# Gate and up projections of an fp32 decoder layer by Strassen's seven products in place of eight, on one core

## The chip, the cores and the metric

The kernel runs on one core of a Trainium2 chip. The metric is the device time of one execution in microseconds (us). Before the change the median of three runs is 1079.65 us (1079.23 to 1080.08). Engines: PE (TensorE, matmuls and transposes), DVE (VectorE), ACT (ScalarE), POOL (GpSimd), SP (SyncE, which issues the DMAs of the kernel before).

## What is computed

One layer of a decoder on 1024 tokens of width 1024, all in fp32; the channel mixer has 2816 columns.

```python
h = x * (1 + sc1) + sh1
z = h @ w_in + b_in
y = concat([short_conv, pooling, conformer, S5](z)) @ w_o
x = layer_norm(ALPHA * x + (1 + g1) * y, ln1_g, ln1_b)
h = x * (1 + sc2) + sh2
f = (silu(h @ w_gate) * (h @ w_up)) @ w_down
x = layer_norm(ALPHA * x + (1 + g2) * f, ln2_g, ln2_b)
```

The six vectors sc1 to g2 come from a small product with the conditioning vector (`ada`). Layer norms reduce over the 1024 columns of a token.

## The kernel before

**Products.** An fp32 operand is held as two fp32r parts: `split` (L80, L81) makes the high part with an ACT cast and the low part with a DVE subtraction. `passes` (L130 to L132) multiplies two such operands in three matmuls: high by high, high by low, low by high. A matmul is 128 rows by 128 by 512 columns wherever gate, up and down are concerned, and one instruction each.

**Tiles.** The tokens go in two halves of 512 (c = 0, 1). Gate and up have 22 tiles f of 128 columns. `gate_up(c, f, h2)` loads and splits two weight tiles (`gu_pairs`), multiplies both with the modulated input h2 over all 8 row blocks of 128 (`gu_mm`: 2 x 8 x 3 = 48 matmuls into two PSUM banks), and `gu_act` takes silu of one (L593, ACT) times the other (L594, DVE) and splits the result into an act tile that stays in SBUF until the down projection. `down(c)` multiplies 22 act tiles with w_down into eight PSUM banks (528 matmuls).

**Order.** Most of the program is written inside `in_order(ON_PE)`, so PE works in the order of the text; a scheduler sets the order of the other engines by their inputs and priorities. The first half's output projection and norm (`ln1(0, t)`, t = 0 to 3, token tiles of 128) come first. Then gate and up tiles 0 to 10 of the first half (GU_FIRST = 11) run on PE while DVE makes the 31 conformer taps (L408) and other mixers of the second half, T3 = 8 taps per tile. The second half's output projection follows (`out_proj1`, eight PSUM banks, `res1` L529 and L530 reads them), then tiles 11 to 14 of the first half, one ahead of each `ln1(1, t)`, and 15 to 21, then `down(0)`, the 22 tiles of the second half, and `down(1)`.

**ln1.** Statistics on DVE (L476, L479), 1 / deviation by a chain of ten small operations on POOL (`rsqrt`, L376 to L394, and L537), the normalised rows r on ACT (L539), eight transposes on PE (L546) into two PSUM banks, and eight 128-wide ACT operations (L556) that scale and shift them into the next input. For c = 0 the result is split into h2 at once; for c = 1 it goes to DRAM (h2_d) and is loaded and split ahead of the second half's tiles. `keep_x1` scales r (L567, L568) and stores it for `res2`.

**Buffers.** Loads go through four 4 KB-a-partition tiles (tag `raw`); `tmp` has three. Weight pairs (`pr`) rotate through a list; big tiles share space by tag (`ha`, `hb0` to `hb7`, `y0` to `y7`, `m0` to `m5`).

## Time and profile before

| what | value |
|---|---|
| median of 3 runs | 1079.65 us |
| span of the profiled execution | 1076.1 us |
| PE busy | 1040.0 us (97%) |
| DVE busy | 609.1 us (57%) |
| ACT busy | 328.4 us (31%) |
| POOL busy | 142.2 us (13%) |
| DMA issues by POOL | none |

The span is 3.55 us below the median of the runs; the difference lies around the span and is taken to stay. Matmuls overlap, so the time that one costs is read from start to start, not from its own duration. A share of busy time is an average over stages. [...]

### The profile page before, as it was taken

Reading aid. Unit: us, or ns where it says so; the run is one execution under the profiler, and the core shown is the slowest. Engines: PE = TensorE matmul, PEld = TensorE weight load, DVE = VectorE, ACT = ScalarE, POOL = GpSimd, SP = SyncE. Lnnn points to the kernel's source line nnn. Section 1 sums busy time; section 2 is a strip of 40 time slices with the busy share of each in tenths; the row PEclk is TensorE's granted clock in tenths of the full one; section 3 lists DMA queues with packets and bytes.
Section 4 is the critical chain, followed back from the end, with each engine's and each line's share of the span. In section 5 each row is a group of like instructions: output and inputs, shape, how many; then the busy total and the mean of one; then the engine's idle time right before and its main releaser. Section 6 shows DMA issues by size and latency. Waiting matters only on the chain.

```text
span 1076.1 us, 12408 instructions
## 1 busy us (share of the span) xinstructions
PE 1040.0 (97%) x4744; PEld 846.5 (79%) x4744; DVE 609.1 (57%) x921; ACT 328.4 (31%) x462; POOL 142.2 (13%) x447
## 2 busy tenths in 40 slices
PE   8959999999999999999999999999999999999995
PEld 7747777678888888888788888888888888888884
...
DMA packets 53963, 145.23 MB, mean 135 GB/s; under 512 B 9296, under 2 KB 17520, under 8 KB 53904
## 3 DMA queue, kind: packets, MB, share of 16 engines
...
q8 instruction: 37, 0.61, 0.2%
...
## 4 chain that ended last, share of the span: by engine, by line
PE 67%; POOL 9%; DVE 8%; issue 8%; DMA 5%; ACT 2%; SPq 0%; DVEq 0%; POOLq 0%; ACTq 0%
PE mm L131 20%; PE mm L130 19%; PE mm L132 19%; DMA raw<-in_w_ada_dram 2%; POOL s L855 2%; POOL s L862 2%; PE sm L130 2%; PE sm L131 2%; PE sm L132 2%; DMA raw<-in_w_up_dram 2%; DVE raw L168 1%; PE sm L1119 1%; POOL rs_a L376 1%; ACT tmp L556 1%; DVE pr L81 1%
## 5 line engine op out<-in xcount | busy, mean ns | idle before, releaser
L81 DVE TENSOR_TENSOR pr<-raw,pr 128x1024 fp32r<-128x1024 f32 (+1 forms) x161 | 192.1, 1196 | 268.7 <-ACT pr L80 268.3
L130 PE MATMUL mm<-h,pr 128*128 128x512 f32 (+1 forms) x736 | 281.9, 383 | 0.0
L131 PE MATMUL mm<-h,pr 128*128 128x512 f32 (+1 forms) x736 | 280.8, 382 | 0.2 <-DVE h L81 0.2
L132 PE MATMUL mm<-h,pr 128*128 128x512 f32 (+1 forms) x736 | 279.8, 380 | 0.6 <-DVE pr L81 0.5
L80 ACT CAST pr<-raw 128x1024 fp32r<-128x1024 f32 (+1 forms) x161 | 164.9, 1027 | 368.8 <-PE sm L132 130.2
L132 PEld LDWEIGHTS mm<-h,pr 128*128 128x128 f32 x736 | 138.3, 188 | 28.6 <-DVE pr L81 1.5
L130 PEld LDWEIGHTS mm<-h,pr 128*128 128x128 f32 x736 | 138.3, 188 | 27.8 <-issue 0.5
L131 PEld LDWEIGHTS mm<-h,pr 128*128 128x128 f32 x736 | 138.4, 188 | 26.8 <-issue 0.5
L376 POOL TENSOR_SCALAR rs_a<-lmv 128x1 f32<-128x1 f32 x16 | 12.0, 750 | 697.4 <-DVE lmv L479 695.9
L130 PE MATMUL mm<-pr,act 128*128 128x512 f32 x240 | 94.3, 393 | 0.0
L132 PE MATMUL mm<-pr,act 128*128 128x512 f32 x240 | 94.2, 392 | 0.0
L131 PE MATMUL mm<-pr,act 128*128 128x512 f32 x240 | 94.1, 392 | 0.0
L408 DVE SCALAR_TENSOR_TENSOR acc<-up,pack,acc 128x512 f32<-128x512 f32 x120 | 85.0, 747 | 0.0
L594 DVE TENSOR_TENSOR tmp<-tmp,mm 128x512 f32<-128x512 f32 x44 | 30.1, 685 | 71.5 <-PE mm L132 65.1
L168 DVE SCALAR_TENSOR_TENSOR raw<-raw,cond 128x1024 f32<-128x1024 f32 x48 | 58.0, 1222 | 15.8 <-DMA raw<-in_w_ada_dram 15.8
L593 ACT ACTIVATE tmp<-mm 128x512 f32<-128x512 f32 x44 | 26.2, 600 | 118.8 <-PE mm L132 118.8
L131 PE MATMUL mm<-h_a,pr 128*128 128x512 f32 x104 | 42.7, 411 | 13.7 <-DVE h_a L81 13.7
L132 PEld LDWEIGHTS mm<-pr,act 128*128 128x128 f32 x240 | 45.0, 188 | 10.3
L131 PEld LDWEIGHTS mm<-pr,act 128*128 128x128 f32 x240 | 45.1, 188 | 10.3
L130 PEld LDWEIGHTS mm<-pr,act 128*128 128x128 f32 x240 | 45.0, 188 | 10.2
L130 PE MATMUL mm<-h_a,pr 128*128 128x512 f32 x104 | 42.9, 413 | 2.1 <-ACT h_a L80 2.1
L132 PE MATMUL mm<-h_a,pr 128*128 128x512 f32 x104 | 42.1, 405 | 0.0
...
## 6 DMA issues: line engine op xcount, KB each, us to landing
raw<-in_w_ada_dram SPq DMA_DIRECT2D x48, 512.0 KB, 5.0
raw<-in_w_gate_dram SPq DMA_DIRECT2D x44, 512.0 KB, 3.3
raw<-in_w_up_dram SPq DMA_DIRECT2D x44, 512.0 KB, 3.4
raw<-in_w_down_dram SPq DMA_DIRECT2D x44, 512.0 KB, 3.2
raw<-in_w_o_dram SPq DMA_DIRECT2D x16, 512.0 KB, 3.4
raw<-in_w_inB_dram SPq DMA_DIRECT2D x10, 512.0 KB, 3.5
raw<-in_x_dram SPq DMA_DIRECT2D x8, 512.0 KB, 3.2
x_d<-r SPq DMA_DIRECT2D x8, 512.0 KB, 3.5
```

The source lines that it names most:

```text
L80: S.copy(hi, src)
L81: V.tensor_tensor(out=lo, in0=src, in1=hi.bitcast(F32), op=SUB)
L130: PE.matmul(o, wh, xh, start=first, stop=False)
L131: PE.matmul(o, wh, xl, start=False, stop=False)
L132: PE.matmul(o, wl, xh, start=False, stop=last)
L168: V.scalar_tensor_tensor(out=w, in0=w, scalar=1.0, in1=cond, op0=MUL, op1=MUL, accum_out=mod[:, j:j + 1])
L376: G.tensor_scalar(out=a, in0=v, scalar1=EPS, scalar2=None, op0=ADD)
L408: V.scalar_tensor_tensor(out=o, in0=u, scalar=dww[:, i, j:j + 1], in1=o, op0=MUL, op1=ADD)
L593: S.activation(g[:, :CH], z[0], AF.Silu)
L594: V.tensor_tensor(out=g[:, :CH], in0=g[:, :CH], in1=z[1], op=MUL)
L855: i = e.tensor_tensor(out=o, in0=a, in1=b, op=op)
L862: self.eng(o).tensor_scalar(out=o, in0=a, scalar1=s1, scalar2=s2, op0=op0, **kw)
```

## The change

For gate, and likewise for up, let A be the weights of two column tiles (2j, 2j+1) by the two halves of the 1024 rows, and B the two halves of the rows by the two halves of the tokens. Four blocks of output take eight block products; the change takes seven (the Winograd form). A block product for gate and up together is 2 x 4 x 3 = 24 matmuls.

- **On the first half of the tokens:** `c11(j)` takes two of the products, p1 = A11 x B11 and A12 x B21. Their sum is the first half's tile 2j, whose act goes to DRAM (`act_d`). ACT copies p1 out of PSUM between the two products (L616), in the middle of an accumulation, and it is stored (`p1_d`). Tiles 2j + 1 of the first half are not computed here. `c11` runs for j = 0 to 7 ahead of the second half's output projection (GU_FIRST = 8, CF = 6, T3 = 10) and for j = 8 to 10 ahead of `ln1(1, 0)` to `ln1(1, 2)`.
- **When the second half has its norm:** `strassen(j)`, j = 0 to 10, takes the other five products (s1 x t1, s4 x B22, s2 x t2, s3 x t3, A22 x t4; 120 matmuls). `a_ops` loads four weight tiles and makes the sums of weights on DVE (L685) and five split operands; DVE combines p1 and PSUM into the three other blocks (L710 to L730), reading a bank in the middle of its accumulation; acts go to DRAM.
- **Sums of inputs:** `ln1(1, t)` makes the split operands t1 and B22 itself (`tb`), loading B11 from DRAM, and stores t1. `t_ops` loads inputs and t1 back from DRAM and makes t2, t3 and t4 (12 operands, 12 subtractions and 12 splits) behind the first two products of j = 0.
- **Around it:** acts of both halves are loaded from DRAM in the down stage (`down_ops`), the scaling of x1 moves there (`keep_x1`), and x_d, h_d, t_d, p_d and act_d are written by 64 DMAs that POOL issues. SP issues 346 DMAs (317 before). The g, b rows move later, h_b becomes two tiles.

128x512 matmuls: 4144 before, 3880 after. DVE TENSOR_TENSOR operations: 548 and 811. ACT casts: 258 and 318, copies 22 and 48.

```diff
-GU_FIRST = 11
-CF = 8
-T1, T2, T3 = 6, 2, 8
+GU_FIRST = 8
+CF = 6
+T1, T2, T3 = 6, 2, 10
...
     def ln1(c, t, r, h2):
...
         S.activation(r, r, AF.Identity, scale=rs, bias=nb)
+        G.dma_start(x1_d[c * 4 + t], r)
...
-        if c == 1:
-            SP.dma_start(h2_d[:, :, tt].rearrange("k p t -> p k t"), hv)
+        G.dma_start(h2_d[:, :, c * CH + t * P:c * CH + (t + 1) * P].rearrange("k p t -> p k t"), hv)
+        if c == 1:
+            b11 = raw_p.tile([P, 1024], F32, name="raw", tag="raw", bufs=4)
+            bv = b11[:, :CH].rearrange("p (k t) -> p k t", k=4)
+            SP.dma_start(bv, h2_d[:4, :, t * P:(t + 1) * P].rearrange("k p t -> p k t"))
+            V.tensor_tensor(out=bv, in0=hv[:, :4], in1=bv, op=SUB)
+            split(tb[0][:, :4, 0, tt], tb[0][:, :4, 1, tt], bv)
+            split(tb[1][:, :, 0, tt], tb[1][:, :, 1, tt], hv[:, 5:])
+            split(tb[0][:, 4, 0, tt], tb[0][:, 4, 1, tt], hv[:, 4])
+            G.dma_start(t1_d[:, :, tt].rearrange("k p t -> p k t"), bv)
...
+    def product(o, w, m, b, first, last, hs=slice(0, CH)):
+        for k in range(4):
+            ks = slice(512 * m + k * P, 512 * m + (k + 1) * P)
+            xh, xl = B[b][k]
+            passes(o, (w[:, 0, ks], w[:, 1, ks]), (xh[:, hs], xl[:, hs]), first and k == 0, last and k == 3)
+    def c11_mm(w, z, p1, q, lo=0, n=CH):
+        hs = slice(lo, lo + n)
+        for i in range(2):
+            product(z[i][:, hs], w[i], q, ("11", "21")[q], q == 0, q == 1, hs)
+            if q == 0:
+                S.copy(p1[:, i * CH + lo:i * CH + lo + n], z[i][:, hs])
+    def c11_act(j, z, p1):
+        G.dma_start(p1_d[j].rearrange("p a t -> p (a t)"), p1)
+        g = tmp()
+        S.activation(g[:, :CH], z[0], AF.Silu)
+        V.tensor_tensor(out=g[:, :CH], in0=g[:, :CH], in1=z[1], op=MUL)
+        G.dma_start(act_d[2 * j][:, :CH], g[:, :CH])
...
+    def t_ops():
...
+        for k in range(4):
+            a, b = [raw_p.tile([P, 1024], F32, name="raw", tag="raw", bufs=4) for _ in range(2)]
+            SP.dma_start(a[:, :CH], t1_d[k])
+            SP.dma_start(b, h2_d[4 + k])
+            SP.dma_start(a[:, CH:], h2_d[k][:, CH:])
+            V.tensor_tensor(out=a[:, :CH], in0=b[:, CH:], in1=a[:, :CH], op=SUB)
+            put("t2", a[:, :CH])
+            V.tensor_tensor(out=b[:, CH:], in0=b[:, CH:], in1=a[:, CH:], op=SUB)
+            put("t3", b[:, CH:])
+            V.tensor_tensor(out=b[:, :CH], in0=b[:, :CH], in1=a[:, :CH], op=SUB)
+            put("t4", b[:, :CH])
...
+    def strassen(j):
+        w = a_ops(j)
...
+        for m in range(2):
+            product(Z[m], w["s1"], m, "t1", True, False)
+            V.tensor_tensor(out=c22[m], in0=P1[m], in1=Z[m], op=ADD)
+        for m in range(2):
+            product(Z[m], w["s4"], m, "22", False, True)
+            V.tensor_tensor(out=c12[m], in0=P1[m], in1=Z[m], op=ADD)
+        yield
+        X = [mm() for _ in range(2)]
+        for m in range(2):
+            product(X[m], w["s2"], m, "t2", True, False)
+            V.tensor_tensor(out=c12[m], in0=c12[m], in1=X[m], op=ADD)
+        S.activation(c12[0], c12[0], AF.Silu)
+        V.tensor_tensor(out=c12[0], in0=c12[0], in1=c12[1], op=MUL)
+        G.dma_start(act_d[2 * j][:, CH:], c12[0])
+        for m in range(2):
+            product(X[m], w["s3"], m, "t3", False, False)
+            V.tensor_tensor(out=c22[m], in0=c22[m], in1=X[m], op=ADD)
+        for m in range(2):
+            product(X[m], w["22"], m, "t4", False, True)
+            V.tensor_tensor(out=c21[m], in0=P1[m], in1=X[m], op=ADD)
+            if m == 0:
+                S.activation(hi[0], hi[0], AF.Silu)
+        V.tensor_tensor(out=hi[0], in0=hi[0], in1=hi[1], op=MUL)
+        G.dma_start(act_d[2 * j + 1], hi[0])
...
     for t in range(4):
-        gate_up(0, f, h2)
+        if f < FT // 2:
+            c11(f)
+            f += 1
         run(ln1(1, t, rr[t], None))
...
+    with in_order(ON_PE):
+        for j in range(FT // 2):
+            st = strassen(j)
+            run(st, 1)
+            if j == 0:
+                t_ops()
+            run(st)
+            if j == 2:
+                for i in range(40, 48):
+                    ada(i)
```

**ACT around the first norm of the second half.** Before, in the order of ACT's queue from the silu of tile 11 on (r_3779, r_3797 are the rows of token tiles 0 and 1; lnb and lrs come from POOL; `waits` lists the engines or DMA queues whose semaphores an instruction waits for):

```order
L593 ACTIVATE tmp<-mm 128x512 [waits PE_49]
L539 ACTIVATE r_3779<-r_3779,lnb,lrs 128x1024 [waits DVE_49,Pool_49]
L80 CAST pr<-raw 128x1024 [waits DMAHW7_49,DVE_49]
L539 ACTIVATE r_3797<-r_3797,lnb,lrs 128x1024 [waits DVE_49,Pool_49]
L80 CAST pr<-raw 128x1024 [waits DMAHW0_49,PE_49,Activation_49]
L80 CAST act<-tmp 128x512 [waits DVE_49]
L556 ACTIVATE tmp<-mm,hB,hA 128x128 [waits PE_49]
L556 ACTIVATE tmp<-mm,hB,hA 128x128 x3
L556 ACTIVATE tmp<-mm,hB,hA 128x128 [waits PE_49]
L556 ACTIVATE tmp<-mm,hB,hA 128x128 x3
L539 ACTIVATE r_3815<-r_3815,lnb,lrs 128x1024 [waits Pool_49]
L539 ACTIVATE r_3833<-r_3833,lnb,lrs 128x1024 [waits DVE_49,Pool_49]
```

In the change, at the same place, from the first copy of p1 of `c11(8)` on (p_3662 is its p1, p_3782 that of `c11(9)`; r_3590, r_3608, r_3626 are the rows of token tiles 0 to 2):

```order
L616 COPY p_3662<-mm 128x512 [waits DMASW6_49,DMAHW5_49,DVE_49,PE_49]
L558 ACTIVATE r_3590<-r_3590,lnb,lrs 128x1024 [waits Pool_49]
L616 COPY p_3662<-mm 128x512 [waits PE_49]
L80 CAST pr<-raw 128x1024 [waits DMAHW5_49]
L621 ACTIVATE tmp<-mm 128x512 [waits PE_49]
L80 CAST pr<-raw 128x1024 [waits DMAHW6_49]
L558 ACTIVATE r_3608<-r_3608,lnb,lrs 128x1024 [waits DVE_49,Pool_49]
```

and directly behind these, with the scalings and casts of token tile 0 (tb is the operand they make):

```order
L576 ACTIVATE tmp<-mm,hB,hA 128x128 [waits DMASW7_49,PE_49]
L576 ACTIVATE tmp<-mm,hB,hA 128x128 x3
L576 ACTIVATE tmp<-mm,hB,hA 128x128 [waits PE_49]
L576 ACTIVATE tmp<-mm,hB,hA 128x128 x3
L80 CAST tb<-raw 128x4x128 [waits DVE_49]
L80 CAST tb<-tmp 128x3x128 [waits Activation_49]
L80 CAST tb<-tmp 128x128
L616 COPY p_3782<-mm 128x512 [waits DMASW4_49,PE_49]
L558 ACTIVATE r_3626<-r_3626,lnb,lrs 128x1024 [waits Pool_49]
L616 COPY p_3782<-mm 128x512 [waits PE_49]
```

Each second copy of p1, for which PE waits in the middle of a tile, now stands behind the rows of a token tile, which wait for POOL; the first copy of `c11(9)` also stands behind the eight scalings and three casts of token tile 0.

**POOL at the same place.** In the change, from the last operation for token tile 0 on (rs_a_3844 begins the chain of token tile 1, rs_a_3964 that of 2):

```order
L556 TENSOR_SCALAR lnb<-lmv,lrs 128x1 [waits Pool_49]
L382 TENSOR_SCALAR rs_a_3844<-lmv 128x1 [waits DVE_49]
L383 TENSOR_SCALAR lrs<-rs_a_3844 128x1 [waits Pool_49]
L387 TENSOR_SCALAR rs_b_3845<-lrs,rs_a_3844 128x1 [waits Pool_49]
L392 TENSOR_SCALAR rs_c_3846<-rs_b_3845 128x1 [waits Pool_49]
L559 DMA x_d<-r_3590 128x1024 [waits DMAHW1_49,DMASW0_49,DMAHW4_49,PE_49,Activation_49]
L619 DMA p_d<-p_3662 128x1024 [waits DMASW1_49,Activation_49]
L394 TENSOR_SCALAR rs_b_3845<-rs_c_3846,rs_b_3845 128x1 [waits Pool_49]
L382 TENSOR_SCALAR rs_a_3964<-lmv 128x1 [waits DVE_49]
L400 TENSOR_TENSOR lrs<-lrs,rs_b_3845 128x1 [waits Pool_49]
L383 TENSOR_SCALAR lrs<-rs_a_3964 128x1 [waits Pool_49]
L387 TENSOR_SCALAR rs_b_3845<-lrs,rs_a_3844 128x1 [waits Pool_49]
```

Before, the four chains stand one behind the other with no DMA between; now the stores of x_d and p_d stand inside the chain of token tile 1, and wait for ACT.

**DVE at the start of the first `strassen`.** In the change, from the last low parts of `tb` on (pr are the weight operands, room holds p1 and sums of weights, bop are the operands of `t_ops`):

```order
L81 TENSOR_TENSOR tb<-raw,tb 128x4x128 [waits Activation_49]
L81 TENSOR_TENSOR tb<-tmp,tb 128x3x128 [waits Activation_49]
L81 TENSOR_TENSOR tb<-tmp,tb 128x128 [waits Activation_49]
L81 TENSOR_TENSOR pr<-raw,pr 128x512 [waits Activation_49] x4
L81 TENSOR_TENSOR pr<-room,pr 128x512 [waits Activation_49] x2
L81 TENSOR_TENSOR pr<-raw,pr 128x512 [waits Activation_49]
L710 TENSOR_TENSOR tmp<-room,mm 128x512 [waits DMAHW0_49,DMASW5_49,PE_49]
L649 TENSOR_TENSOR raw<-raw 128x512 [waits DMAHW3_49,DMAHW2_49,DMASW6_49]
L653 TENSOR_TENSOR raw<-raw 128x512 [waits DMASW0_49,DVE_49]
L651 TENSOR_TENSOR raw<-raw 128x512 [waits DMAHW4_49]
L81 TENSOR_TENSOR bop<-raw,bop 128x512 [waits Activation_49]
L710 TENSOR_TENSOR tmp<-room,mm 128x512 [waits DMASW7_49,DMASW1_49,PE_49]
```

Nothing like it stood there before; the loads that L649 to L653 wait for follow, by way of DRAM, on stores that POOL issues after the last token tile's operands.

## Rows read from the trace of the kernel before

**Rows 1.** The page: busy time and share of the span, instructions.

```profile
PE 1040.0 (97%) x4744; PEld 846.5 (79%) x4744; DVE 609.1 (57%) x921; ACT 328.4 (31%) x462; POOL 142.2 (13%) x447
```

**Rows 2.** Waits of PE: line waited for by whom, us in total, times, longest.

```profile
PE mm L131 <- DVE h_a L81: 13.7, 3, 12.6
PE mm L546 <- ACT r L539: 2.5, 2, 2.0
```

**Rows 3.** Instructions of L594, 740 to 945 us: duration min/median/max, first and last start.

```profile
L594 DVE TENSOR_TENSOR tmp<-tmp,mm x19: 687/689/689, 746.3 to 943.1; 128x512 f32<-128x512 f32 x19
```

**Rows 4.** Groups of DVE by form, 300 to 700 us: busy, mean ns, idle before.

```profile
L81 DVE TENSOR_TENSOR pr<-raw,pr 128x1024 fp32r<-128x1024 f32 x71 | 86.5, 1222 | 120.5 <-ACT pr L80 120.3
L408 DVE SCALAR_TENSOR_TENSOR acc<-up,pack,acc 128x512 f32<-128x512 f32 x50 | 34.6, 745 | 0.0
...
L81 DVE TENSOR_TENSOR act<-tmp,act 128x512 fp32r<-128x512 f32 x22 | 15.1, 686 | 1.7 <-ACT act L80 1.6
```

**Rows 5.** Groups of ACT by form, 300 to 1076 us, same columns.

```profile
L80 ACT CAST act<-tmp 128x512 fp32r<-128x512 f32 x44 | 27.2, 619 | 28.3 <-DVE tmp L594 28.0 <-DVE acc L408 0.2
L593 ACT ACTIVATE tmp<-mm 128x512 f32<-128x512 f32 x44 | 26.2, 600 | 118.8 <-PE mm L132 118.8
```

**Rows 6.** Timeline of DVE: start us, us, operation, idle before and releaser.

```profile
298.94 0.69 DVE L81 TENSOR_TENSOR h<-tmp,h 128x512 fp32r<-128x512 f32 x1 [1.37 <-ACT h L80]
...
313.18 2.73 DVE L408 SCALAR_TENSOR_TENSOR acc<-up,pack,acc 128x512 f32<-128x512 f32 x4
```

**Rows 7.** Timeline of PE: last matmul of the output projection, first of tile 11.

```profile
455.17 0.39 PE L132 MATMUL sm<-pr,ys 128*128 128x512 f32 x1
455.39 0.39 PE L130 MATMUL mm<-h,pr 128*128 128x512 f32 x1
```

**Rows 8.** Timeline of ACT around the second half's norm.

```profile
465.32 1.25 ACT L539 ACTIVATE r<-r,lnb,lrs 128x1024 f32<-128x1024 f32 x1 [2.87 <-POOL lnb L537]
...
469.49 1.24 ACT L539 ACTIVATE r<-r,lnb,lrs 128x1024 f32<-128x1024 f32 x1 [1.99 <-POOL lnb L537]
...
472.09 2.89 ACT L556 ACTIVATE tmp<-mm,hB,hA 128x128 f32<-128x128 f32 x8
```

**Rows 9.** Timeline of POOL: first and last operations of two chains of ten.

```profile
470.75 0.21 POOL L376 TENSOR_SCALAR rs_a<-lmv 128x1 f32<-128x1 f32 x1 [1.30 <-ACT r L539]
...
476.87 0.26 POOL L537 TENSOR_SCALAR lnb<-lmv,lrs 128x1 f32<-128x1 f32 x1
477.22 0.21 POOL L376 TENSOR_SCALAR rs_a<-lmv 128x1 f32<-128x1 f32 x1
...
480.18 0.26 POOL L537 TENSOR_SCALAR lnb<-lmv,lrs 128x1 f32<-128x1 f32 x1
```

**Rows 10.** Timeline of PE: eight transposes and what follows.

```profile
387.70 1.04 PE L424 MATMUL sm<-ident,acc 128*128 128x128 f32 x8
388.50 0.48 PE L130 MATMUL mm<-h,pr 128*128 128x512 f32 x1
```

**Rows 11.** DMA issues: engine, count, KB each, median us to landing.

```profile
x_d<-r SPq DMA_DIRECT2D x8, 512.0 KB, 3.5
...
h_d<-tmp SPq DMA_DIRECT2D x4, 512.0 KB, 5.6
raw<-h_d SPq DMA_DIRECT2D x8, 256.0 KB, 2.6
```

**Rows 12.** Timeline of PE behind its longest wait.

```profile
67.26 0.80 PE L131 MATMUL mm<-h_a,pr 128*128 128x512 f32 x1 [12.63 <-DVE h_a L81]
...
71.61 0.39 PE L132 MATMUL sm<-h_a,pr 128*128 128x512 f32 x1
```

**Rows 13.** Windows: length, busy time (instructions) of PE, PEld, DVE, ACT, POOL, granted clock, DMA.

```profile
310.00:370.00 60.00, 60.00 (x262) 48.77 (x261) 59.91 (x86) 17.78 (x23) 0.00 (x0) 1.00 0.34 113
202.00:204.00 2.00, 2.00 (x7) 1.36 (x6) 1.72 (x3) 1.98 (x4) 0.00 (x0) 0.50 0.10 29
285.00:290.00 5.00, 3.16 (x27) 3.16 (x28) 4.11 (x6) 4.46 (x7) 3.18 (x5) 1.00 0.71 223
```

More of the change, by code (lines that the diff above doesn't have):

```diff
@@ new lines, in trunk, with raw2, a_ops, put @@
+    R_TAGS = ["y6", "y7", "rowa", "rowb"]
+    rcnt = [0]
+    def raw2(src):
+        i = rcnt[0] % 8
+        rcnt[0] += 1
+        if i % 2 == 0:
+            return raw(src)
+        t = yp.tile([P, 1024], F32, name="raw", tag=R_TAGS[i // 2])
+        SP.dma_start(t, src)
+        return t
+    def a_ops(j):
+        ra = [[raw2(A[n][2 * j + b]) for b in range(2)] for n in ("w_gate", "w_up")]
+        s2 = room[:, 2 + j % 2]
+        w = {}
+        def put(name, srcs):
+            pt = pair_tile()
+            for m in range(2):
+                split(pt[:, 0, H[m]], pt[:, 1, H[m]], srcs[m])
+            w[name] = pt
+        a11, a12, a21, a22 = ([ra[m][b][:, H[q]] for m in range(2)] for b in range(2) for q in range(2))
+        s2 = [s2[:, H[m]] for m in range(2)]
+        def op(o, a, b, what):
+            for m in range(2):
+                V.tensor_tensor(out=o[m], in0=a[m], in1=b[m], op=what)
+        op(a21, a11, a21, SUB)
+        op(s2, a22, a21, SUB)
+        op(a11, s2, a11, ADD)
+        put("s1", a11)
+        op(a12, a12, s2, SUB)
+        put("s4", a12)
+        put("s2", s2)
+        put("s3", a21)
+        put("22", a22)
+        return w
@@ new lines, in trunk, with down_ops @@
+    FB = tuple(tuple((f, f + 1) for f in range(n)) + ((n, 22),) for n in (19, 15))
+    dn = {0: {}, 1: {}}
+    def down_ops(c, n):
+        b0, b1 = FB[c][n]
+        w, act = {}, {}
+        more = sl.tile([P, 4, 2, 1024], F32R, name="wd", tag="ha") if b1 - b0 > 3 or c == 1 and n == 0 else None
+        if c == 1 and n == 0:
+            dn["first"] = more
+        for f in range(b0, b1):
+            a = raw_p.tile([P, 1024], F32, name="raw", tag="raw", bufs=4)
+            SP.dma_start(a[:, :CH], act_d[f][:, cs(c)])
+            act[f] = acts[(c * FT + f) % 8]
+            split(act[f][:, 0], act[f][:, 1], a[:, :CH])
+            if c == 1 and n < 4:
+                w[f] = dn["first"][:, n]
+            elif f < b1 - 3:
+                w[f] = more[:, f - b0]
+            else:
+                w[f] = pair_tile()
+            split(w[f][:, 0], w[f][:, 1], raw(A["w_down"][f]))
+        dn[c][n] = w, act
@@ L825, in trunk @@
-    o = down(1)
+    tk = [t[:, i] for t, n in zip(tb, HB) for i in range(n)]
+    B["t1"], B["22"] = ([(t[:, 0], t[:, 1]) for t in ts] for ts in (tk[:4], tk[4:]))
+    room = sl.tile([P, 8, 1024], F32, name="room", tag="ha")
+    with in_order(ON_PE):
[8 more added lines that the diff above has]
+                    ada(i)
@@ new lines, in trunk @@
+    g2row = spread(mod[:, 40:48], "rowa")
+    l2g = row_of("ln2_g_row", yp, "rowb")
+    l2b = row_of("ln2_b_row", yp, "rowc")
+    ag = row_of("ln1_g_row", sl, "m0", ALPHA)
+    ab = row_of("ln1_b_row", sl, "m1", ALPHA)
+    acts = hb_tiles("acts")
+    o0, o1 = {}, {}
+    with in_order(ON_PE):
+        last = len(FB[0]) - 1
+        for n in range(last + 1):
+            down_ops(0, n)
+            if n == last - 1:
+                x1 = [keep_x1(0, t) for t in range(4)]
+            if n == last:
+                for i in range(4):
+                    down_ops(1, i)
+            down_mm(0, n, o0)
+        rr = [yp.tile([P, 1024], F32, name="r2", tag=f"y{4 + t}") for t in range(4)]
+        for t in range(4):
+            run(res2(o0, t, rr[t], x1[t]))
+        for n in range(len(FB[1])):
+            if n > 3:
+                down_ops(1, n)
+            down_mm(1, n, o1)
+            if 3 < n < 8:
+                run(ln2(0, n - 4, rr[n - 4]))
+            if n == 8:
+                x1 = [keep_x1(1, t) for t in range(4)]
```

199 lines of the change are left out of this document (93 added, 106 removed).

## The prediction

> **What bounds the kernel now.** I read the page's totals first: PE is busy 97% of the span, DVE 57% [rows 1]. The waits of PE come next; its longest is 12.6 us ahead of the mixers' first product, and at the second half's norm it waits 2.5 us in all [rows 2]. So the time is PE's queue plus a few starts, and a change is worth the matmuls that it takes out less the waits that it puts between those left. The source view of L594 gives the price of a matmul: 19 such multiplications, one per gate and up tile, start from 746.3 to 943.1 us [rows 3], so 18 tiles take 196.8 us, 10.93 us each, 0.228 us for each of 48 matmuls. The span is 1076.1 us and the median of the runs 1079.65 us; I sum against the span and add the same 3.55 us. A measurement of this kernel can tell about 0.2%, 2.2 us, from no change.
>
> **What goes.** 4144 - 3880 = 264 matmuls by 0.228 us: **60.1 us less on PE**, if it stays fed.
>
> **What must stay hidden.** One `strassen(j)` is 120 matmuls, 27.3 us. DVE does 31 operations of 512 columns and one of 1024 in it: 31 x 0.686 + 1.22 = 22.5 us [rows 4]. ACT does ten casts at 0.62 and two silu, 0.60 and at most 1.25: 8.1 us [rows 5, 8]. Both fit beside PE, DVE with 4.8 us to spare, and in the conformer stage DVE was busy 59.91 of 60 us without a pause of PE [rows 13], so a full DVE alone is no bound. Cover gone, each us per iteration would cost 11 us. The casts and low parts of acts, removed from the mixer stage (0.69 us of DVE per tile), pay for the two more taps of T3. The down stage has the matmuls it had, more loads, and x1's scaling; I take zero there, since each act tile feeds 24 matmuls, 5.5 us, and asks of DVE one weight split (1.22) and one act split (0.69). The end behind the last matmul keeps its operations.
>
> **What is added: waits of PE.** PE's order is fixed, and the queues shown ahead tell who stands in front of what it needs. E is the end of the second half's output projection.
>
> - `c11(2)`: its weights' low parts stand behind 15 taps and the two multiplications of tiles 0 and 1. The last low part of h2 ends near 299.6, four taps take 2.73 us [rows 6]; 15 take 10.2, the multiplications wait until silu has run behind the second tile's matmuls, and the split takes 1.22. PE has 96 narrow matmuls, half as wide, so 10.9 us. About 2.4 us late.
> - `c11(7)`: the second copy of p1 stands behind four ACT operations that wait for the conformer's POOL chain: 0 to 4 us, I take 0.8.
> - `c11(8)`: the second copy stands behind the rows of token tile 0. Before, those began at 465.32 with E = 455.39 [rows 7, 8], at E + 9.9; they take 1.25 and the copy 0.6, so E + 11.8. PE needs the copy after 36 matmuls, at E + 8.2, and starts 0.2 late. **3.5 us** in all.
> - `c11(9)`: POOL's two stores for tile 8 wait for that copy, and the chain of token tile 1 goes on behind them. A chain of ten takes 3.2 us alone (477.22 to 480.44) and 6.4 beside DVE work (470.75 to 477.13) [rows 9]; what is left is about eleven operations of two chains, 3.5 to 7 us. Then rows (1.24), eight scalings (2.89) [rows 8], a subtraction and three casts, then the first copy: E + 22.2 to 25.7, while PE wants it at E + 20.9. 1.3 to 4.8 us; I take 3.7, nearer the upper row, as DVE is at work there.
> - `c11(10)`: its weights' load waits for a slot and for the store of t1; 1.1 us, with 0 to 3 as bounds.
> - **First `strassen`:** its first product needs t1 of all 512 tokens, but the transposes of token tiles 2 and 3 follow `c11(10)`. From there ACT begins when eight transposes are done, 0.8 us [rows 10], and does eight scalings (2.9), the casts (0.62 + 0.45 + 0.2) behind DVE's subtraction (0.69), the same again for tile 3, and a weight's cast and low part (1.3): 0.8 + 2 x 4.9 + 1.3 = 11.9. Less 1.6 us of transposes that is about 10.3; with the semaphores between I take **10.8 us** idle.
> - **t2 of the first `strassen`:** the last inputs go out by POOL and come back. A store like it took 5.6 us to landing, a load 2.6 [rows 11], so `t_ops` begins some 6 us after the first product does. Then 29 DVE operations stand ahead of the last t2, most at 0.61 to 0.69: ready about 18 to 20 us later, 36 us after `c11(10)`, where PE wants it 27 us after. **9.6 us**, and 2.1 us before that, since the first read of the second bank (L710) stands behind three subtractions that wait for the loads.
> - Elsewhere in the beginning (h_b in two tiles): 0.5 us.
>
> Together 34.5 us.
>
> **The clock.** Behind the wait of 12.6 us, ten matmuls took from 67.26 to 71.61 us, 4.35 us where 2.28 is usual [rows 12]. Behind a wait of 2.4 us the granted clock was 0.50, the lower level, at 202 to 204 us, and with waits of 2.0 and 0.5 us it stayed 1.00 at 285 to 290 [rows 13]. I add 2.1 us for each of the two long waits and nothing for the short ones, which stand among dense matmuls like those at 285; as upper bound 1.7 us for each of four. So 4.2 us.
>
> **A store issued by POOL has no row here** (before has none). The nearest are SP's, 3.5 and 5.6 us to landing, and POOL's own chains, which doubled beside DVE. I take what SP's take, and as upper bound 3.2 us more for each store on the path, the difference of the two chains. That gives nothing to the sum and 9.6 us for the three stores on the path (two ahead of token tile 1's chain, one ahead of `t_ops`). [...]
>
> **Sum:** -60.1 + 34.5 + 4.2 = -21.4 us on the span: 1054.7, with 3.55 us around it **1058 us**.
>
> **Rivals.**
>
> *The waits are mostly hidden.* The bounds below: `c11(7)`, `c11(10)` and `c11(2)` nothing, `c11(9)` 1.3, and operands of the first `strassen` made more closely (DVE at 0.61 us, the loads early) 14 instead of 22.5, no clock term: some 19 us, 1079.65 - 60.1 + 19 = 1038 us; with the first slow store landing early as little as 1033. For it: such chains overlapped well at 465 to 495 us, where PE waited for rows 2.5 us only. Against: there nothing of PE's accumulation hung on them.
>
> *Stores by POOL are late beside DVE.* 9.6 us more, 1068 us. For it rows 9; against, only three stores lie on the path.
>
> *Slower: every `strassen` iteration waits.* PE comes back to a bank after one other product, 12 matmuls or 2.7 us; by then DVE must have read it (six such reads: L710, L713, L718, L724 and those of the next j). If a read stands behind a low part whose ACT cast or weight sum is not ready, it is late by up to a cast and a low part, 0.62 + 0.69 = 1.3 us. The point from which it decides is 21.4 / 11 = 1.95 us per iteration, 0.33 us per read. At half of 1.3 us per read it costs 6 x 0.65 x 11 = 43 us: 1101 us. For it: the order of DVE puts one to four operations ahead of reads, weight sums among them; against: 4.8 us of DVE are free per iteration, and weights come an iteration early.
>
> *No gain from fewer matmuls.* If the matmuls that interleave with reads of their bank run slower by 60 / 1320, 0.045 us each, the saving is lost; nothing in the trace shows a matmul above 0.23 us in a full queue, so it has little weight.
>
> **Chances.** The forecast, 1045 to 1065 us, 0.50; hidden, 0.22; late stores, 0.14; every iteration late, 0.11, of which 0.01 ends within 0.2%; no gain 0.03, of which 0.02 within. So faster 0.86, same 0.03, slower 0.11. The range from 1034 to 1076 us takes in the lower bounds, the stores at their upper price and the clock's upper bound (1058 + 6.8 + 9.6), and leaves out the slower cases and a few hundredths below.
>
> **What would show it.** Right: steps of 0.228 us through the eleven iterations; PE waits of some 3.5 us each for L616 copies in `c11(8)` and `c11(9)`; about 10 us before the first matmul on tb and 10 us before the last t2 operand; a low clock behind both. Wrong: repeated waits of PE for DVE in every iteration (slower), waits for tb and bop of 2 to 4 us (hidden), or POOL's DMA issues taking more than 1 us each. The step that I trust least is the length of the two queues in the first `strassen`, 22.5 us of the sum.

## The result, and the profile after

The changed kernel takes 1062.33 us in the median of 4 runs (1059.58 to 1067.08), the kernel before 1079.87 us (1079.23 to 1080.71, 4 runs) beside it: a ratio of 0.984, with a 95% interval of 0.981 to 0.987. That is faster by more than the 0.2% that can be told, 4.3 us above the forecast of 1058 us, and inside the range. The profiled execution took 1061.97 us, its span is 1060.2 us, 15.9 us less than the span before.

The first view is the page's busy times, which answer to [rows 1]:

```profile
PE 996.3 (94%) x4480; PEld 803.8 (76%) x4480; DVE 739.1 (70%) x1184; ACT 344.2 (32%) x537; POOL 177.8 (17%) x511
```

PE has 264 instructions less, as counted, DVE 263 more. PE's share fell from 97% to 94%: it now waits more. The waits of PE, by line waited for (us in total, times, longest; [rows 2] before):

```profile
PE mm L131 <- DVE h_a L81: 14.5, 4, 13.5
PE mm L130 <- ACT pr L80: 9.4, 2, 8.4
PE mm L130 <- ACT bop L80: 5.8, 2, 3.2
PE mm L130 <- ACT p L616: 3.7, 3, 2.6
PE mm L130 <- DVE c L718: 3.2, 1, 3.2
PE mm L130 <- ACT ys L80: 3.2, 1, 3.2
PE mm L132 <- DVE pr L81: 2.8, 2, 1.9
```

The first line was there before. The second is mostly the first product on tb (8.4 of its 9.4 us), the third and part of others the t2 operands, the fourth the copies of p1: the places of the forecast. The fifth and sixth were not forecast. Of the seventh, 0.93 us stand at `c11(2)`, as forecast; the other 1.90, at 289.89 us, are for the low part of a weight of `c11(0)` and were not forecast.

Four marks on PE divide the two spans: the first matmul with 256 columns (the start of `c11(0)`; before, of tile 0), the end E of the second half's output projection, the last matmul of the down stage, and the end. They are read from these starts, in the timeline of PE before,

```profile
281.78 0.28 PE L130 MATMUL mm<-h,pr 128*128 128x256 f32 x1
...
1064.62 0.40 PE L132 MATMUL sm<-pr,act 128*128 128x512 f32 x1
```

with E at 455.39 from [rows 7], and after:

```profile
286.17 0.28 PE L130 MATMUL mm<-h,pr 128*128 128x256 f32 x1
...
431.33 0.39 PE L130 MATMUL mm<-h,pr 128*128 128x512 f32 x1
...
1048.44 0.39 PE L132 MATMUL sm<-pr,acts 128*128 128x512 f32 x1
```

A loss is the difference of a stretch plus what the matmuls that went out of it, at 0.228 us each [rows 3], would have saved (144 of them between the first two marks, 120 behind E):

| stretch | before | after | difference | by matmuls | loss | forecast loss |
|---|---|---|---|---|---|---|
| to `c11(0)` | 281.8 | 286.2 | +4.4 | 0 | **4.4** | 0.5 |
| `c11(0)` to E | 173.6 | 145.2 | -28.4 | -32.8 | **4.4** | 3.2 |
| E to the last matmul | 609.2 | 617.1 | +7.9 | -27.3 | **35.2** | 35.0 |
| behind it | 11.5 | 11.8 | +0.3 | 0 | **0.3** | 0 |

So 60.1 us went and 44.2 came back, where 38.7 were forecast. Behind E the total is the forecast's, but made up otherwise. The timeline of PE, where a bracket holds the idle time before and its releaser:

```profile
441.12 0.50 PE L130 MATMUL mm<-h,pr 128*128 128x512 f32 x1 [0.87 <-ACT p L616]
...
453.12 0.54 PE L130 MATMUL mm<-h,pr 128*128 128x512 f32 x1 [2.59 <-ACT p L616]
...
482.44 0.79 PE L130 MATMUL mm<-tb,pr 128*128 128x512 f32 x1 [8.40 <-ACT pr L80]
...
487.67 0.39 PE L130 MATMUL mm<-tb,pr 128*128 128x512 f32 x1
...
501.52 0.79 PE L130 MATMUL mm<-bop,pr 128*128 128x512 f32 x1 [3.23 <-ACT bop L80]
...
506.44 0.79 PE L130 MATMUL mm<-bop,pr 128*128 128x512 f32 x1 [2.54 <-ACT bop L80]
...
574.05 0.76 PE L130 MATMUL mm<-bop,pr 128*128 128x512 f32 x1 [3.19 <-DVE c L718]
```

With some shorter ones (0.23 ahead of the first, 0.56, 0.36 and 0.49 around the two on bop) PE stood 22.5 us behind E, not 30.8. The rest of the 35.2, 12.7 us, is for the most part a lower clock behind the waits: the slow steps there, each counted beyond 0.228 us and its idle time, come to about 11.7 us; the last 1 us was not placed. Twelve steps from 482.44 to 487.67 took 5.2 us, where 2.7 is usual. The windows (length, busy time of PE, PEld, DVE, ACT, POOL, granted clock as a part of full speed, DMA) show it behind four waits, and its absence from the iterations:

```profile
317.00:319.00 2.00, 1.85 (x4) 1.49 (x5) 2.00 (x4) 0.00 (x0) 0.00 (x0) 0.50 0.85 295
484.00:486.00 2.00, 2.00 (x6) 1.56 (x5) 2.00 (x4) 1.50 (x3) 0.00 (x0) 0.50 0.63 162
508.00:510.00 2.00, 2.00 (x5) 1.53 (x5) 1.89 (x4) 0.31 (x1) 0.00 (x0) 0.50 0.76 211
576.00:578.00 2.00, 2.00 (x6) 1.54 (x5) 2.00 (x4) 0.00 (x0) 0.00 (x0) 0.50 0.78 279
600.00:700.00 100.00, 100.00 (x436) 81.57 (x435) 71.16 (x110) 27.33 (x44) 4.33 (x8) 1.00 0.35 123
```

Two causes stand in the queues of other engines. For the wait at 574 us, DVE's timeline:

```profile
570.17 0.69 DVE L685 TENSOR_TENSOR raw<-raw 128x512 f32<-128x512 f32 x1 [4.15 <-DMA raw<-in_w_gate_dram]
571.41 0.69 DVE L685 TENSOR_TENSOR raw<-raw 128x512 f32<-128x512 f32 x1 [0.55 <-DMA raw<-in_w_up_dram]
572.02 1.29 DVE L685 TENSOR_TENSOR room<-raw 128x512 f32<-128x512 f32 x2
573.22 0.68 DVE L718 TENSOR_TENSOR c<-c,mm 128x512 f32<-128x512 f32 x1
```

L718 reads the bank that PE needs. It stands behind sums of the next iteration's weights (L685), and these wait for loads; at this point, j = 2, the eight loads of `ada` share the slots. For the ys wait, ACT's timeline:

```profile
235.27 1.04 ACT L80 CAST pr<-raw 128x1024 fp32r<-128x1024 f32 x1 [11.73 <-DMA raw<-in_w_o_dram]
236.22 2.17 ACT L80 CAST ys<-y 128x512 fp32r<-128x512 f32 x4
```

Four casts for the first half's output projection stand behind the cast of a weight whose load comes late; PE waits 3.15 us for them and 1.16 for the low part. Before, two of these casts ran at 229.61 us, ahead of that weight's cast, and only two behind it (235.99).

### The profile page after: what moved, and what is told of

Read it like the earlier page. It is cut to its first block, busy times and chain, and to the rows that moved or that the text cites. A ratio compares the mean times of both kernels' runs of the same rounds, so it can differ in the third digit from the quotient of the medians.

```text
span 1060.2 us, 12508 instructions
## 1 busy us (share of the span) xinstructions
PE 996.3 (94%) x4480; PEld 803.8 (76%) x4480; DVE 739.1 (70%) x1184; ACT 344.2 (32%) x537; POOL 177.8 (17%) x511
## 4 chain that ended last, share of the span: by engine, by line
PE 67%; DVE 12%; POOL 10%; DMA 5%; issue 4%; ACT 1%; SPq 0%; DVEq 0%; POOLq 0%
PE mm L132 19%; PE mm L131 19%; PE mm L130 19%; POOL s L1021 2%; PE sm L130 2%; PE sm L132 2%; PE sm L131 2%; POOL s L1028 2%; DMA raw<-in_w_ada_dram 2%; DVE acc L414 1%; DVE raw L168 1%; DVE pr L81 1%; DMA raw<-h_d 1%; DMA raw<-in_w_up_dram 1%; PE sm L1285 1%
## 5 line engine op out<-in xcount | busy, mean ns | idle before, releaser
L81 DVE TENSOR_TENSOR pr<-raw,pr 128x512 fp32r<-128x512 f32 (+1 forms) x179 | 164.9, 935 | 88.1 <-ACT pr L80 87.7
L80 ACT CAST pr<-raw 128x512 fp32r<-128x512 f32 (+1 forms) x179 | 141.8, 821 | 256.1 <-PE mm L132 83.9
L130 PE MATMUL mm<-bop,pr 128*128 128x512 f32 x264 | 106.5, 403 | 9.0 <-ACT bop L80 5.8
L131 PE MATMUL mm<-bop,pr 128*128 128x512 f32 x264 | 106.1, 402 | 1.4 <-DVE bop L81 1.4
L132 PE MATMUL mm<-bop,pr 128*128 128x512 f32 x264 | 105.7, 400 | 0.0
L131 PE MATMUL mm<-pr,acts 128*128 128x512 f32 x216 | 84.7, 392 | 0.0
L130 PE MATMUL mm<-pr,acts 128*128 128x512 f32 x216 | 84.6, 392 | 0.0
L132 PE MATMUL mm<-pr,acts 128*128 128x512 f32 x216 | 84.6, 392 | 0.0
L130 PE MATMUL mm<-h,pr 128*128 128x512 f32 (+1 forms) x208 | 77.0, 370 | 4.6 <-ACT p L616 3.7
L132 PE MATMUL mm<-h,pr 128*128 128x512 f32 (+1 forms) x208 | 75.7, 365 | 2.8 <-DVE pr L81 2.8
L130 PE MATMUL mm<-tb,pr 128*128 128x512 f32 x176 | 70.0, 398 | 8.4 <-ACT pr L80 8.4
L131 PE MATMUL mm<-h,pr 128*128 128x512 f32 (+1 forms) x208 | 75.4, 363 | 0.0
L131 PE MATMUL mm<-tb,pr 128*128 128x512 f32 x176 | 69.7, 396 | 0.0
L132 PE MATMUL mm<-tb,pr 128*128 128x512 f32 x176 | 69.5, 395 | 0.0
L130 PEld LDWEIGHTS mm<-bop,pr 128*128 128x128 f32 x264 | 50.8, 193 | 22.5 <-ACT bop L80 6.9
L131 PEld LDWEIGHTS mm<-bop,pr 128*128 128x128 f32 x264 | 50.8, 193 | 14.5 <-DVE bop L81 2.8
L132 PEld LDWEIGHTS mm<-bop,pr 128*128 128x128 f32 x264 | 50.7, 192 | 11.7
L131 PE MATMUL mm<-h_a,pr 128*128 128x512 f32 x104 | 42.1, 404 | 14.5 <-DVE h_a L81 14.5
L80 ACT CAST acts<-raw 128x512 fp32r<-128x512 f32 x44 | 27.2, 620 | 74.2 <-DMA raw<-act_d 64.0
```

The source lines that it names most:

```text
L80: S.copy(hi, src)
L81: V.tensor_tensor(out=lo, in0=src, in1=hi.bitcast(F32), op=SUB)
L130: PE.matmul(o, wh, xh, start=first, stop=False, skip_group_check=True)
L131: PE.matmul(o, wh, xl, start=False, stop=False, skip_group_check=True)
L132: PE.matmul(o, wl, xh, start=False, stop=last, skip_group_check=True)
```

## The experiments

**Theories.** A: PE's waits come from places in the in-order queues of ACT and DVE, that is from operations standing ahead that wait for a norm, a load or another operand; what a wait costs is its idle time and a lower clock behind it. B, the rival: from the transport (stores that POOL issues, and the way through DRAM), or from DVE being too busy in the iterations. Kernels e1 to e4, e5 to e7 with e0, and e9 to e11 ran on one chip each, e12 on another; the kernel before took 1083.7, 1081.97, 1084.12 and 1083.98 us there, so kernels are compared by their ratio to it, or by stretches of their traces. e0 is the changed kernel again; from `c11(0)` to the down stage its stretches differ from the first trace's by 0.1 us at most, and its ratio of 0.982 beside the first 0.984 shows that a difference of 0.002 means nothing. The stretches, in us of one trace each: beginning (to `c11(0)`), from the start of the output projection's last matmul (0.23 us ahead of E) to the first matmul on tb, from there to the down stage.

| kernel | median (range) | ratio, 95% | beginning | E to tb | tb to down |
|---|---|---|---|---|---|
| e0 changed, again | 1061.17 (1059.87 to 1063.43) | 0.982 [0.979, 0.984] | 285.7 | 51.4 | 323.6 |
| e1 ada late | 1063.01 (1061.23 to 1063.65) | 0.982 [0.980, 0.985] | 290.9 | 51.3 | 319.6 |
| e2 SP stores | 1065.48 (1059.81 to 1069.03) | 0.984 [0.980, 0.989] | 286.5 | 53.0 | 322.6 |
| e3 room | 1057.34 (1057.03 to 1058.07) | 0.977 [0.975, 0.980] | 286.8 | 51.3 | 316.8 |
| e4 fill | 1063.63 (1061.78 to 1066.49) | 0.983 [0.981, 0.986] | 288.8 | 51.4 | 324.7 |
| e5 one more ahead | 1065.30 (1063.17 to 1067.31) | 0.985 [0.983, 0.987] | 287.2 | 61.1 | 321.0 |
| e6 ys apart | 1055.65 (1054.18 to 1060.18) | 0.977 [0.974, 0.980] | 285.1 | 51.4 | 321.4 |
| e7 more DVE | 1058.08 (1057.54 to 1058.75) | 0.979 [0.977, 0.980] | 287.1 | 51.3 | 318.0 |
| e9 t2 first | 1055.01 (1053.81 to 1055.78) | 0.973 [0.971, 0.975] | 289.1 | 51.2 | 314.1 |
| e10 transposes inside | 1063.44 (1059.79 to 1065.68) | 0.980 [0.978, 0.983] | 289.2 | 48.6 | 326.2 |
| e11 together | 1050.74 (1049.47 to 1055.04) | 0.970 [0.967, 0.972] | 286.1 | 48.7 | 318.7 |
| e12 three edits | 1051.99 (1050.82 to 1052.20) | 0.970 [0.969, 0.972] | 285.8 | 51.3 | 313.7 |

**e0**, the changed kernel again.

> The changed kernel as it is, beside the other three on the same chip. Theory A (its time is fixed from the end of the output projection on and varies in the beginning, where waits hang on loads): from the first matmul on tb to the last one of the down stage within 1 us of 566 us, the narrow matmuls' start anywhere from 284 to 291 us, median 1060 to 1064 us.

The table's first row is the measure for the others.

**e1**: the eight `ada` behind j = 2 go one behind each of j = 2 to 9.

```diff
-            if j == 2:
-                for i in range(40, 48):
-                    ada(i)
+            if 2 <= j < 10:
+                ada(38 + j)
```

> One part moved: the eight small products of ada that stand behind the iteration j = 2 are taken one each behind j = 2 to 9. Theory A (a read of a PSUM bank by DVE stands behind weight sums whose loads the eight ada loads made late): the wait of 3.2 us for L718 at 574 us goes, and with it the stretch at the lower clock behind it (2.9 us), so about 6 us less than the changed kernel, 1056 us, and no other wait takes its place. Rival B (DVE as a whole is full in the iterations, the wait only shows where): the same DVE work is still there, the wait moves to another iteration and the time stays within 1.5 us.

The wait of 3.2 us at j = 2 is gone, and the stretch is 4.0 us shorter. One wait of 1.15 us for L718 stands at 740.70 us instead. The whole is no faster; in this trace the beginning was 4.7 us longer than in the first trace of the changed kernel (the wait for ys 4.4 us). So without the loads of `ada` at j = 2 the wait at 574 goes. They are not its whole cause: e3 and e7 below lose it too, with `ada` in its place. And the beginning moves by as much as this edit gains.

**e2**: SP issues the second half's stores of h_d and t_d.

```diff
-        G.dma_start(h2_d[:, :, c * CH + t * P:c * CH + (t + 1) * P]...
+        (G, SP)[c].dma_start(h2_d[:, :, c * CH + t * P:c * CH + (t + 1) * P]...
-            G.dma_start(t1_d[:, :, tt]...
+            SP.dma_start(t1_d[:, :, tt]...
```

> One part undone: the second half's stores of h_d and t_d are issued by SP, as h_d was before the change, in place of POOL. Theory A (POOL's stores are as quick as SP's: 3.3 to 3.8 us to landing in the changed kernel): within 2 us of the changed kernel, a little slower if a store that waits in SP's queue holds back loads behind it. Rival B (stores by POOL are late beside DVE, as the prediction's third case has it): the loads of t_ops start earlier by 3 us or more and the time falls by 3 to 8 us.

No gain: E to tb 1.6 us longer, the stretch behind 1.0 shorter. The page's DMA issues (KB each, median us to landing) of the changed kernel,

```profile
h_d<-tmp POOLq DMA_DIRECT2D x8, 512.0 KB, 3.8
...
t_d<-raw POOLq DMA_DIRECT2D x4, 256.0 KB, 4.0
```

and of e2, for the same stores:

```profile
h_d<-tmp SPq DMA_DIRECT2D x4, 512.0 KB, 3.8
...
t_d<-raw SPq DMA_DIRECT2D x4, 256.0 KB, 3.4
```

The transport part of B falls as far as the issuing engine goes.

**e3**: the loads of `t_ops` for k = 0 and 1 go into free parts of room and wait for no slot of raw.

```diff
+            if k < 2:
+                a, b = room[:, 4 + 2 * k], room[:, 5 + 2 * k]
+            else:
+                a, b = [raw_p.tile([P, 1024], F32, name="raw", tag="raw", bufs=4) for _ in range(2)]
```

> One part of the changed kernel: the first two of the four steps of t_ops load into space that lies free in the tile room, so that all four steps have buffers at once. Theory A (the waits for t2 in the first iteration come from load buffers that are given back one by one, not from the way through DRAM): the waits of 3.2 and 2.5 us for bop go or fall under 1 us each, and the stretch at the lower clock behind them shrinks; 6 to 9 us less, 1054 to 1056 us. Rival B (the way through DRAM, or DVE's queue of 24 operations, sets it): the waits keep at least 5 of their 7.2 us, time within 2 us of the changed kernel.

6.8 us less behind tb, but the waits for bop fell only from 7.2 to 5.5 us; nearly all of the rest is that the wait at j = 2 vanished, presumably because the loads behind now fall into other slots (not shown). DVE's timeline shows what keeps t2 late:

```profile
502.40 0.68 DVE L654 TENSOR_TENSOR raw<-raw 128x512 f32<-128x512 f32 x1
...
503.61 0.69 DVE L656 TENSOR_TENSOR raw<-raw 128x512 f32<-128x512 f32 x1
...
504.81 0.69 DVE L652 TENSOR_TENSOR raw<-raw 128x512 f32<-128x512 f32 x1
```

The last t2 (L652) starts at 504.81, behind a t3 (L654) and a t4 (L656) that are needed some 24 and 48 matmuls later.

**e9**: e3, and three loops: all of t2, then t3, then t4.

```diff
+            ab.append((a, b))
+        for a, b in ab:
             V.tensor_tensor(out=a[:, :CH], in0=b[:, CH:], in1=a[:, :CH], op=SUB)
             put("t2", a[:, :CH])
+        for a, b in ab:
             V.tensor_tensor(out=b[:, CH:], in0=b[:, CH:], in1=a[:, CH:], op=SUB)
...
```

> The earlier variant of t_ops with room for all loads, and beside it one order changed: all four t2 operands are made ahead of those of t3 and t4. In that variant DVE worked without a pause from 491 to 508 us and still made the last t2 at 505 us, behind subtractions for t3 and t4 that nobody wants yet. Theory A (with buffers enough, the order of t_ops sets the wait for t2): the waits for bop fall from 5.5 us to under 2.5 and the stretch from the first matmul on tb to the down stage from 316.8 to 311 to 314 us. Rival B (the way of t1 and h through DRAM sets it, since the first subtraction began at 491.4 us, 7.7 us behind the first product): waits stay above 4 us, the stretch within 1.5 us of 316.8.

The waits of PE for bop, 5.5 us in e3, are now 2.3 us:

```profile
PE mm L130 <- ACT bop L80: 1.7, 1, 1.7
...
PE mm L131 <- DVE bop L81: 0.6, 2, 0.4
```

That is theory A shown for t2: without a shorter transfer, the order alone took most of the wait away, and the ratio is 0.973 against 0.977.

**e4**: nine useless fp32 products behind the last transposes (`ident` by `cond` into a spare bank; 18 records in the trace), whose result nothing uses.

```diff
+        run(ln1(1, 3, rr[3], None))
+        fill = sm()
+        for _ in range(9):
+            PE.matmul(fill, ident, cond[:, :CH], start=True, stop=True)
```

> Added work: nine fp32 matmuls of no use between the last transposes and the first matmul on tb, some 7 us on PE where it waits 8.4 us. Nothing else differs, the output is the same. Theory A (PE at the lower clock behind this place because it was idle): the granted clock stays at 1.00 at 484 to 490 us, the first twelve matmuls on tb take 2.7 us in place of 5.2, and the time falls by about 2.5 us. Rival B (the lower clock has another cause, such as the load of the whole chip, or the first matmul of an operand is slow in itself): still 0.50 behind it, time the same or up to 1 us more.

PE's timeline:

```profile
477.11 7.89 PE L958 MATMUL sm<-cond,ident 128*128 128x512 f32 x18
...
485.65 0.51 PE L130 MATMUL mm<-tb,pr 128*128 128x512 f32 x1 [0.65 <-ACT pr L80]
```

and the window behind it:

```profile
488.00:490.00 2.00, 2.00 (x10) 1.66 (x9) 2.00 (x5) 0.71 (x2) 0.00 (x0) 1.00 0.69 202
```

With PE kept at work the clock stays 1.00 behind tb, where it was 0.50: PE had stood 8.40 us there, and in e4 0.65. The 2 us gained are given back at the waits behind, and the stretch is 1.1 us longer than in e0: counted from the first matmul on tb, the last wait for t2 ends only 0.9 us earlier than in e0 (the waits for bop are 8.2 us in all, from 7.2), and the wait for L718, at 577.87 us, is 3.87 us, from 3.06. So the clock behind the tb wait was real, and worth nothing by itself.

**e10**: the transposes of token tiles 2 and 3 go inside `c11(10)`, one ahead of each half (gate, up) of its second block product.

```diff
+        c11_mm(w, z, p1, 0)
+        run(ln[0])
+        product(z[0], w[0], 1, "21", False, True)
+        run(ln[1])
+        product(z[1], w[1], 1, "21", False, True)
```

> One part of the changed kernel moved: the transposes of token tiles 2 and 3 stand inside the last two-product tile (behind its first product, and between the two halves of its second) in place of behind it. Same operations. Theory A (the 8.4 us ahead of the first matmul on tb are ACT's scalings and casts for two token tiles with nothing on PE beside them): half of a tile, 5.5 us of matmuls, now runs beside them; from the end of the output projection to the first matmul on tb 46 to 48 us in place of 51.3. Rival B (the copies of p1 of that tile now stand behind the scalings, and PE waits there instead, as it did where one more tile was left for this place): 50 us or more.

The wait for tb fell to 5.75 us, and E to tb is 2.7 us shorter; the stretch behind is 2.6 us longer. Counted from the first matmul on tb, the last wait for t2 ends 1.4 us later than in e0, and the wait for L718, at 576.13 us, grew from 3.06 to 4.33 us: these took it all.

**e5**: one tile fewer ahead of the second half's norm (GU_FIRST 7, CF 5, T3 13), so that `c11(7)` to `c11(10)` cover it.

```diff
-GU_FIRST = 8
-CF = 6
-T1, T2, T3 = 6, 2, 10
+GU_FIRST = 7
+CF = 5
+T1, T2, T3 = 6, 2, 13
```

> One size changed: seven of the two-product tiles stand ahead of the second half's output projection in place of eight (the conformer's products behind the fifth, 13 taps per tile), so that one stands ahead of each of the four token tiles of the second half's norm and the transposes of token tile 2 no longer follow the last one. Theory A (8.4 us of waiting ahead of the first matmul on tb are ACT's and DVE's work on two token tiles that has no matmuls beside it): one token tile's share, 4 to 5 us, goes; from the end of the narrow matmuls to the first matmul on tb 163 to 165 us in place of 168.2. Rival B (the mixers of the second half have no room to lose 10.9 us of matmuls): the output projection starts late and the same stretch takes 168 us or more.

The wait for tb fell from 8.40 to 5.58 us. But the copy of p1 now meets the conformer's chain, in ACT's timeline

```profile
371.05 1.94 ACT L442 ACTIVATE tmp<-sm,cnb,crs 128x256 f32<-128x256 f32 x4 [5.13 <-POOL cnb L439]
372.86 1.08 ACT L616 COPY p<-mm 128x512 f32<-128x512 f32 x2
```

and on PE:

```profile
373.51 0.79 PE L130 MATMUL mm<-h,pr 128*128 128x512 f32 x1 [2.87 <-ACT p L616]
```

From the last narrow matmul to the first on tb it took 109.2 + 61.1 = 170.3 us, against 116.9 + 51.4 = 168.3. A wait of the kind forecast for `c11(7)` (0 to 4 us), which did not come there, comes in this order.

**e6**: the first operand ys of the first half's output projection gets a tile of its own.

```diff
-            ys = ys0[0][:, n]
+            ys = sl.tile([P, 2, CH], F32R, name="ys", tag="tmp", bufs=3) if n == 0 else ys0[0][:, n]
```

> One part undone: the first operand of the first half's output projection has a tile of its own again in place of a slice of the merged tile. Theory A (the wait of 3.15 us for ys at 237 us, 0.98 before, comes from the merged h_b tiles: its cast stands behind a weight cast that waits for its load): the wait for ys by ACT goes below 1 us and the narrow matmuls begin some 3 to 5 us earlier, at 281 to 283 us (286.2 in the changed kernel). Rival B (the projection's start is late because its loads are): still 2 us or more of waiting there, and the narrow matmuls begin within 1 us of 286 to 291 us.

The wait for ys is gone, but PE waits 2.2 us in its place for an activation that empties a bank (y, L802) behind the same weight's cast and the casts of the other ys, and the beginning is only 0.6 us shorter than e0's. The median is 5.5 us lower than e0's all the same; the profiled execution, at 1060.18, was the slowest of the four, so where the other three gain was not seen.

**e7**: eight useless additions more on DVE in each iteration from j = 1.

```diff
+        if j:
+            for _ in range(4):
+                V.tensor_tensor(out=room[:, 7, :CH], in0=cond[:, :CH], in1=cond[:, CH:], op=ADD)
```

(ahead of the products with s2, and again ahead of those with A22)

> Added work: eight DVE additions of 512 columns of no use in each iteration j = 1 to 10, 8 x 0.61 to 0.69 = 4.9 to 5.5 us of DVE per iteration. Theory A (the iterations have DVE to spare, 7 to 8 us of 27.3 by the changed kernel's trace at 600 to 700 us, so nothing but the order of its queue can hold PE up): the stretch from the first matmul on tb to the down stage, 323.6 us, grows by under 5 us. Rival B (the prediction's slower case: reads of PSUM have less than 0.7 us to spare each, so that every operation put in front of one shows): 10 iterations by 1.3 to 3 us, 13 to 30 us longer.

```profile
600.00:700.00 100.00, 100.00 (x436) 81.61 (x435) 98.31 (x156) 27.33 (x44) 4.12 (x8) 1.00 0.38 128
```

In this window of e7 DVE is busy 98.31 of 100 us and PE still without a pause; the same window had 71.16 before the edit. The rival "every iteration waits" falls, with room to spare. The kernel is even shorter: the wait for L718 is gone, as in e3. So that wait does not hang on how busy DVE is; that it hangs on how loads fall into slots is the likely reason, and was not shown.

**e11** is e6, e9 and e10 together, **e12** the same without e10.

> Four edits together: the first operand of the first output projection apart, room for all loads of t_ops, t2 first, the transposes of token tiles 2 and 3 inside the last two-product tile. Theory A (the losses are separate waits in PE's queue, so their gains add): against the changed kernel's 1061 to 1062 us some 5 (operand apart), 4 to 7 (room), 3 to 5 (t2 first) and 3 to 5 (transposes) less: 1042 to 1048 us. Rival B (what is gained ahead of one wait is given back at the next, as with the added matmuls, since t2 waits for DVE whatever PE does): 1050 us or more.

> The edits together without the moved transposes: the first operand of the first output projection apart, room for all loads of t_ops, t2 first. Theory A (these three losses are separate, and moving the transposes only brought the wait for t2 forward): the stretch from the first matmul on tb to the down stage within 2 us of 314, from the output projection's end to it 51.3; 4 us less than with the moved transposes in the first of these, 1047 to 1051 us, and a ratio of 0.967 to 0.971. Rival B (the operand apart gave nothing that lasts, its gain goes to the next wait in the beginning): 1053 us or more, ratio 0.973 as without it.

Both reach a ratio of 0.970, 1.2 to 1.4% below the changed kernel (0.982 and 0.984) and 3% below the kernel before. The gains do not add up to the 1042 to 1048 us of e11's theory A; e12 came out at the ratio forecast for it, 1 us above the time. e10's 2.6 us at tb are given back at t2 once more: PE's waits for bop are 6.3 us in e11 and 2.4 in e12 (e11's trace is of the slowest of its four executions, 1055.04 us). The three edits of e12 give as much as four and are the version to keep.

## Why the prediction came out right, point by point

- **What goes: right.** 264 matmuls at 0.228 us, 60.1 us; the stretches fall by that less the waits.
- **What must stay hidden: right for the iterations, wrong for j = 2.** From 580 us to the down stage PE had no wait at a clock of 1.00, and DVE had less to do than the 22.5 us forecast: 71.16 of 100 us in the window at 600 are 19.4 us of 27.3. e7 shows that even the free time was not needed. But the bound "cover gone" was put on DVE's time alone. The step that failed is that weights "come an iteration early": at j = 2 the loads of `ada` take their slots and a read of PSUM stands behind them, 3.2 us and some 3 of lower clock. e1 takes the wait away by moving these loads; e3 and e7 lose it without, so it is no fixed price of them.
- **`c11(2)`, `c11(7)`: about right together, in part by luck**, 4.4 us from `c11(0)` to E for 3.2. At `c11(2)` PE waited 0.96 and 0.93 us and then ran at 0.50 (some 1.6 us); at `c11(7)` it did not wait. The 1.90 us at `c11(0)` were not forecast, and neither was that PE waits for rows of the first half 1.3 us, where it was 2.5 before [rows 2].
- **`c11(8)` to `c11(10)`: right in kind, too long.** 1.1, 2.6 and 0 us where 3.5, 3.7 and 1.1 stood. The copies of p1 wait behind rows of token tiles, as the order shows; but the rows of tile 0 came at E + 8.0 (439.36 on ACT), not E + 9.9, since POOL's chain ahead took 3.2 us, the shorter time of [rows 9], although DVE was busy 5.66 of 6 us beside it (434 to 440). ACT's timeline:

```profile
439.36 1.24 ACT L558 ACTIVATE r<-r,lnb,lrs 128x1024 f32<-128x1024 f32 x1 [4.48 <-POOL lnb L556]
440.51 0.56 ACT L616 COPY p<-mm 128x512 f32<-128x512 f32 x1
```

  That the two waits are due to this order was read from the queue and the trace; no run changed it.
- **First `strassen`: right in kind, 15.6 us for 22.5.** tb 8.40 for 10.8, t2 7.2 for 9.6, the read of the second bank 0 for 2.1. Of the t2 wait, the order of DVE's operations makes 3.2 us (e9 against e3) and the buffers of the loads 1.7 (e3). The wait for tb fell where matmuls stood beside that work (5.75 us in e10, 5.58 in e5), as its account has it.
- **The clock: the step that failed.** "Nothing for the short ones" does not hold: the clock was 0.50 behind waits of 0.96 and 0.93, of 2.6 and of 3.2 us; the 0.87 us at 441 cost nothing of it. The two waits at `c11(2)` did this in e0, e11 and e12 too (0.92 to 1.07 us, and matmuls 0.42 to 0.43 us apart behind them); in e5, e9 and e10 waits of 0.92 to 1.14 us at the same place had matmuls 0.22 to 0.24 us apart behind them (0.33 to 0.35 in the first step), the usual step. The row that the forecast took for short waits covers only the one of 2.0 us: that of 0.5 stands at 293.99 us, outside 285 to 290. Behind E the clock is about 12 of the 12.7 us above, for 4.2, which makes up for the 8.3 us of waits that did not come. The agreement behind E, 35.2 and 35.0, is thus two errors that cancel, and luck.
- **Elsewhere in the beginning: mis-sized**, 4.4 us for 0.5. The merged casts of ys are part of it; the wait depends on when a load of w_o lands (2.8 us in e0's trace, 4.4 in e1's), and e6 only moved it.
- **POOL's stores: right to give them nothing.** The two inside the chain of token tile 1 took 0.62 and 0.53 us on POOL (from 441.01). POOL's timeline for those behind, first with DVE busy 0.79 of 2 us, then (from 476 on) 6 of 6:

```profile
463.48 0.76 POOL L591 DMA_DIRECT2D t_d<-raw  x1 [1.36 <-DVE raw L587]
464.23 0.90 POOL L581 DMA_DIRECT2D h_d<-tmp  x1
...
476.64 0.76 POOL L591 DMA_DIRECT2D t_d<-raw  x1 [1.85 <-DVE raw L587]
477.38 0.90 POOL L581 DMA_DIRECT2D h_d<-tmp  x1
```

  The upper price, 3.2 us more for each store on the path, is not seen: beside DVE's tensor_tensor operations from 476 to 482 us (L685, L587, L81) a store of t_d took the 0.76 us that it took with DVE at rest. The longer chain of [rows 9] has no store in it: there POOL's L386, L394 and L381 took 1.21, 1.04 and 1.32 us, from 471.77, 473.75 and 474.90, each beside a tensor_tensor of 128x1024 on DVE (L81 at 471.70, L567 at 473.57, L568 at 474.77; 1.17 to 1.23 us each), and 0.19, 0.19 and 0.34 in the next chain, with DVE at rest. The chain for token tile 0 in the change ran beside DVE's statistics (L485, L488) and took 3.2 us.
- **The rivals.** "Every iteration waits": refuted (e7). "Late stores": refuted (e2, and the rows above). "No gain from fewer matmuls": refuted by 436 matmuls in 100 us at 600 us, as many as before. "Mostly hidden": the waits were indeed shorter, but the lower clock took the difference.
